# A softmax over the diagonal of a batched product: one joint load, one early maximum, one early read and a fifth store at the end of the kernel

## The chip, the cores and the metric

The kernel runs on one core of one Trainium2 chip. The metric is the device time of one execution in microseconds. The profiled span (from the program's first instruction to its last) is about 2 us shorter than that time. In the lines of profiles, DVE is VectorE, ACT is ScalarE and SP the engine that issues the loads; a q behind the name is the engine's queue, where separate waits stand; "issue" is time in which an engine waited for nothing that the profile shows; L83 is a line of the kernel (here the products by row, with their sums).

## The reference

```python
B, N, D = 8, 4096, 512          # x and y: [8, 4096, 512] float32
gram = np.matmul(x, y.transpose(0, 2, 1))
diag = np.diagonal(gram, axis1=1, axis2=2)
diag = diag - diag.max(axis=-1, keepdims=True)
exp = np.exp(diag)
return exp / exp.sum(axis=-1, keepdims=True)
```

Only the diagonal is wanted: for each of 8 x 4096 rows one dot product of 512 elements, then a softmax over 4096 dots. 134 MB are read and 0.13 MB written.

## The kernel before

Four batches form a set; their 4 x 4096 dots lie in a tile `diag[i]` of 128 partitions (32 to a batch) x 128 columns. A step `t` works on 32 columns ("rows" of x and y in each partition, 64 KB). In the code P is 128 partitions, C 128 columns, R 32 rows of a step, W 2, and G the 32 partitions of a batch. Steps 0 to 5 use large products and reduces. The last two steps use `dots`: one VectorE instruction a row, product and sum together. The last step, which the change is about, loads its rows in pieces of 16, 8, 4, 2, 1, 1.

```python
def largest(out, d):
    nc.vector.tensor_reduce(out=out, in_=d, axis=X, op=Alu.max)

def exps(i, d):                                    # softmax, first half
    mxp = small.tile([P, 1], f32, name=f"mxp{i}")
    largest(mxp, d)
    nmx = over_quadrant(f"nmx{i}", mxp, Alu.max, negate=True)     # over the 32 partitions of a batch
    sump = small.tile([P, 1], f32, name=f"sump{i}")
    nc.scalar.activation(out=res[i], in_=diag[i][:, :C], func=Act.Exp, bias=nmx, scale=1.0, accum_out=sump)
    return sump
# ... normalize(i, sump): sum over the quadrant, reciprocal, multiply res[i] ...

# steps 0 to 5: 30 of the 32 rows are summed by VectorE, the last two (W) by ScalarE:
    sums(t, 0, R - W)
    sums_act(t, R - W, W)
# ...
t += 1                                             # the last step
r0 = 0
for n in (16, 8, 4, 2, 1, 1):
    load_x(t, r0, n)
    load_y(t, r0, n)
    if r0 == 0:
        largest(diag[1][:, C : C + 1], diag[1][:, : C - R])
    if r0 == R - 2:
        largest(diag[1][:, C + 1 :], diag[1][:, C - R : C - 2])
    dots(t, r0, n)
    r0 += n

for p in range(0, P, G):                           # first set, in 4 stores
    nc.sync.dma_start(out=ov[0, p : p + G, :], in_=res[0][p : p + G, :])
normalize(1, exps(1, diag[1][:, C - 2 :]))         # 2 dots and 2 early maxima
nc.scalar.dma_start(out=ov[1], in_=res[1])
```

Transfers take eight completion counters in turn; each issue waits until the transfer eight before it has landed (the last y is issued at 304.05 us; the load eight before it landed at 303.99).

## Time and profile before

| | before |
|---|---|
| time, median of 3 runs at first | 321.22 us |
| profiled span | 319.2 us |
| y of the last step's 16 rows lands | 294.19 us |
| last y row lands | 314.15 us |
| last row's product starts | 314.24 us |
| exponential starts | 315.48 us |
| last multiply ends, last store lands | 316.73, 318.34 us |

Read it from the end: the data stream ends at 314.15 us, and then one chain of small instructions on VectorE and ScalarE and one store lead to 319.2. Beside that chain only the four stores of the first set still land, by 314.89. The lines are shown and read in the prediction below.

### The profile page before, as it was taken

Reading aid. Unit: us, or ns where it says so; the run is one execution under the profiler, and the core shown is the slowest. Engines: PE = TensorE matmul, PEld = TensorE weight load, DVE = VectorE, ACT = ScalarE, POOL = GpSimd, SP = SyncE. Lnnn points to the kernel's source line nnn. Section 1 sums busy time; section 2 is a strip of 40 time slices with the busy share of each in tenths; the row PEclk is TensorE's granted clock in tenths of the full one; section 3 lists DMA queues with packets and bytes.
Section 4 is the critical chain, followed back from the end, with each engine's and each line's share of the span. In section 5 each row is a group of like instructions: output and inputs, shape, how many; then the busy total and the mean of one; then the engine's idle time right before and its main releaser. Section 6 shows DMA issues by size and latency. Waiting matters only on the chain.

```text
span 319.2 us, 318 instructions
## 1 busy us (share of the span) xinstructions
DVE 242.8 (76%) x158; ACT 26.9 (8%) x35; POOL 0.2 (0%) x4
## 2 busy tenths in 40 slices
DVE  0000079994899939999399994999949999993995
ACT  1000030100301003010110103001030100000000
POOL 0000000000000000000000000000000000000000
DMA  9999999999999999999999999999999899999992
GB/s 394 394 394 509 411 394 493 427 394 427 493 394 394 517 402 394 493 427 394 435 485 394 394 517 402 394 493 427 394 427 493 378 411 444 412 452 409 421 410 100
DMA packets 4226, 134.36 MB, mean 421 GB/s; under 512 B 513, under 2 KB 769, under 8 KB 1537
## 3 DMA queue, kind: packets, MB, share of 16 engines
q1 hardware_dynamic: 4080, 134.29, 97.8%
q10 hardware_dynamic: 144, 0.07, 0.1%
q14 instruction: 2, 0.01, 0.0%
HBM read 134.22 MB, written 0.13 MB: 421 GB/s over the span
## 4 chain that ended last, share of the span: by engine, by line
DMA 61%; DVE 36%; issue 2%; SPq 0%; ACT 0%; DVEq 0%; ACTq 0%
DMA ys<-in_y_dram 61%; DVE xs L70 27%; DVE xs L83 5%; DVE diag L73 4%; SPq L63 0%; DVE res L111 0%; ACT res L104 0%; DVE nmx L91 0%; DVE sum L91 0%; DVE rc L110 0%; DVE mxp L97 0%; SPq L66 0%; DVEq L70 0%; DVEq L83 0%; ACTq L104 0%
## 5 line engine op out<-in xcount | busy, mean ns | idle before, releaser
L70 DVE TENSOR_TENSOR xs<-xs,ys 128x13312 f32<-128x13312 f32 x6 | 84.1, 14025 | 67.1 <-DMA ys<-in_y_dram 67.1
L73 DVE TENSOR_REDUCE diag<-xs 128x30 f32<-128x15360 f32 x6 | 96.9, 16153 | 0.2
L83 DVE SCALAR_TENSOR_TENSOR xs<-xs,ys 128x512 f32<-128x512 f32 x64 | 39.7, 686 | 5.5 <-DMA ys<-in_y_dram 5.5
L116 ACT ACTIVATE side<-ys 128x3072 f32<-128x3072 f32 x6 | 16.6, 2764 | 123.6 <-DMA ys<-in_y_dram 123.6
L70 DVE TENSOR_TENSOR xs<-xs,side 128x3072 f32<-128x3072 f32 x6 | 20.1, 3350 | 0.0
L78 ACT ACTIVATE xs<-xs 128x512 f32<-128x512 f32 x12 | 7.5, 621 | 88.2 <-DVE xs L70 88.2
L104 ACT ACTIVATE res<-diag,nmx 128x128 f32<-128x128 f32 x2 | 0.8, 401 | 76.6 <-DVE nmx L91 76.6
L83 DVE DVE_READ_ACCUMULATOR xs<-xs,ys 128x1 f32 x64 | 5.2, 82 | 0.0
L78 ACT ACTIVATION_READ_ACCUMULATOR xs<-xs 128x1 f32 x12 | 2.2, 187 | 0.0
L116 ACT ACT_TABLE_LOAD x1 | 1.3, 1283 | 0.7 <-PEq L162 0.7
L91 DVE TRANSPOSE_TENSOR_REDUCE sum<-sump 128x1 f32<-128x32 f32 x2 | 0.4, 207 | 0.6 <-ACT res L104 0.6
L111 DVE TENSOR_SCALAR res<-res,rc 128x128 f32<-128x128 f32 x2 | 0.6, 286 | 0.1
L97 DVE TENSOR_REDUCE mxp<-diag 128x1 f32<-128x128 f32 (+1 forms) x2 | 0.4, 222 | 0.1
L97 DVE TENSOR_REDUCE diag<-diag 128x1 f32<-128x96 f32 (+1 forms) x2 | 0.4, 218 | 0.1
L91 DVE TRANSPOSE_TENSOR_REDUCE nmx<-mxp 128x1 f32<-128x32 f32 x2 | 0.4, 211 | 0.1
L110 DVE RECIPROCAL rc<-sum 128x1 f32<-128x1 f32 x2 | 0.3, 163 | 0.1
L104 ACT ACTIVATION_READ_ACCUMULATOR res<-diag,nmx 128x1 f32 x2 | 0.4, 187 | 0.0
L162 POOL MEMSET const-uint8-127<- 128x1 uint8 x1 | 0.1, 103 | 0.0
L162 POOL MEMSET const-bfloat16-1.0<- 128x1 bf16 x1 | 0.1, 102 | 0.0
L162 POOL MEMSET const-float32-0.0<- 128x1 f32 x1 | 0.1, 99 | 0.2 <-issue 0.2
L162 POOL MEMSET const-float32-1.0<- 128x1 f32 x1 | 0.1, 99 | 0.0
## 6 DMA issues: line engine op xcount, KB each, us to landing
ys<-in_y_dram SPq DMA_DIRECT2D x3, 4096.0 KB, 15.1
xs<-in_x_dram SPq DMA_DIRECT2D x1, 4096.0 KB, 15.2
xs<-in_x_dram SPq DMA_DIRECT2D x1, 2048.0 KB, 19.7
ys<-in_y_dram SPq DMA_DIRECT2D x1, 2048.0 KB, 20.0
xs<-in_x_dram SPq DMA_DIRECT2D x1, 1024.0 KB, 22.1
ys<-in_y_dram SPq DMA_DIRECT2D x1, 1024.0 KB, 22.6
xs<-in_x_dram SPq DMA_DIRECT2D x1, 512.0 KB, 23.5
ys<-in_y_dram SPq DMA_DIRECT2D x1, 512.0 KB, 23.9
```

Of the source, the lines that this page charges most:

```text
L70: nc.vector.tensor_tensor(out=xt, in0=xt, in1=yt, op=Alu.mult)
L73: nc.vector.tensor_reduce(out=dots_of(t, r0, n), in_=rows(t, r0, n), axis=X, op=Alu.add)
L78: nc.scalar.activation(out=row, in_=row, func=Act.Copy, accum_out=dots_of(t, r, 1))
L83: nc.vector.scalar_tensor_tensor(out=xt, in0=xt, scalar=1.0, in1=ys[:, r, :], op0=Alu.mult, op1=Alu.mult, accum_out=dots_of(t, r, 1),)
L91: nc.vector.tensor_reduce(out=got, in_=column.to_broadcast([P, G]), axis=X, op=op, negate=negate, apply_transpose=True)
L97: nc.vector.tensor_reduce(out=out, in_=d, axis=X, op=Alu.max)
L104: nc.scalar.activation(out=res[i], in_=diag[i][:, :C], func=Act.Exp, bias=nmx, scale=1.0, accum_out=sump)
L110: nc.vector.reciprocal(out=rc, in_=total)
L111: nc.vector.tensor_single_scalar(out=res[i], in_=res[i], scalar=rc, op=Alu.mult)
L116: nc.scalar.activation(out=side, in_=ys[:, R - K :, :], func=Act.Copy)
L162: nc = _bacc.Bacc("TRN2", target_bir_lowering=False, num_devices=1)
```

## The change

The intent is to shorten the end: the x of rows 30 and 31 comes in one load, so that the last row waits for one transfer; the two early maxima become one, so that the final maximum takes three columns; ScalarE reads its own earlier sums once (into a tile `met` that nobody uses), so that its exponential need not wait for them; the first set is stored in five pieces and not in four.

```diff
-    diag = [small.tile([P, C + 2 * i], f32, name=f"diag{i}") for i in range(B // Q)]
+    diag = [small.tile([P, C + i], f32, name=f"diag{i}") for i in range(B // Q)]
@@ the last step
     for n in (16, 8, 4, 2, 1, 1):
-        load_x(t, r0, n)
+        if r0 < R - 1:
+            load_x(t, r0, max(n, 2))
         load_y(t, r0, n)
-        if r0 == 0:
-            largest(diag[1][:, C : C + 1], diag[1][:, : C - R])
         if r0 == R - 2:
-            largest(diag[1][:, C + 1 :], diag[1][:, C - R : C - 2])
+            largest(diag[1][:, C:], diag[1][:, : C - 2])
         dots(t, r0, n)
         r0 += n
 
-    for p in range(0, P, G):
-        nc.sync.dma_start(out=ov[0, p : p + G, :], in_=res[0][p : p + G, :])
+    met = small.tile([P, C - R], f32, name="met")
+    nc.scalar.activation(out=met, in_=diag[1][:, : C - R], func=Act.Copy)
+
+    for p, n in ((0, G), (G, G), (2 * G, G), (3 * G, G // 2), (3 * G + G // 2, G // 2)):
+        nc.sync.dma_start(out=ov[0, p : p + n, :], in_=res[0][p : p + n, :])
```

## The prediction

> **What bounds the kernel now.** I read the page first, for the engines' shares and the DMA row.
>
> ```profile
> span 319.2 us, 318 instructions
> DVE 242.8 (76%) x158; ACT 26.9 (8%) x35; POOL 0.2 (0%) x4
> ...
> DMA  9999999999999999999999999999999899999992
> HBM read 134.22 MB, written 0.13 MB: 421 GB/s over the span
> ```
>
> The DMA engines are at 90% or more in 38 of 40 slices: the kernel is a stream of 134 MB, and VectorE (76%) mostly waits for it. All the change's edits lie in the last step, behind the last loads, so what counts is the end of the chain of waits. The same chain cut to 283 to 317 us:
>
> ```profile
> 283.95 20.04 DMA ys<-in_y_dram
> ...
> 304.05 10.10 DMA ys<-in_y_dram
> 314.15 0.03 issue
> 314.18 0.02 DVEq L83
> 314.20 0.04 issue
> 314.24 0.71 DVE xs L83 x2
> ...
> 315.39 0.02 issue
> 315.41 0.02 ACTq L104
> 315.43 0.05 issue
> 315.48 0.07 ACT res L104
> ```
>
> The last y row lands at 314.15; VectorE's queue spends 0.09 us on two waits, then takes the last row at 314.24. After the negated maximum (315.39), ScalarE's queue spends 0.08 us on a wait before the exponential starts at 315.48. Now the timeline of VectorE over that stretch:
>
> ```profile
> 312.97 0.18 DVE L97 TENSOR_REDUCE diag<-diag 128x1 f32<-128x30 f32 x1
> 313.08 0.68 DVE L83 SCALAR_TENSOR_TENSOR xs<-xs,ys 128x512 f32<-128x512 f32 x1
> 313.68 0.08 DVE L83 DVE_READ_ACCUMULATOR xs<-xs,ys 128x1 f32 x1
> 314.24 0.69 DVE L83 SCALAR_TENSOR_TENSOR xs<-xs,ys 128x512 f32<-128x512 f32 x1 [0.48 <-DMA ys<-in_y_dram]
> ```
>
> VectorE is almost the bound here: it is idle only 0.48 us before the last row. Whatever the DMA gains, no more than about that can be won. Is the last load late because it was issued late? It waited until 304.05 for the landing of the load eight before it (the program has eight completion counters in turn). But the views of DMA issues, one short window each, give for the last four loads:
>
> ```profile
> xs<-in_x_dram SPq DMA_DIRECT2D x1, 256.0 KB, 24.2
> ys<-in_y_dram SPq DMA_DIRECT2D x1, 256.0 KB, 18.6
> xs<-in_x_dram SPq DMA_DIRECT2D x1, 256.0 KB, 14.4
> ys<-in_y_dram SPq DMA_DIRECT2D x1, 256.0 KB, 10.1
> ```
>
> With issues at 288.05, 294.26, 299.15 and 304.05 they land at about 312.21, 312.89, 313.55 and 314.15 (the second decimals from the counters' updates in the trace): one each 0.60 to 0.68 us, however early issued. Even the last stood 10 us in a full queue. Issue time is no constraint.
>
> **What the Trainium skill says.** "DMA: Bandwidth & Descriptors", section "Queues, rings and completion order": on each DMA engine descriptors are consumed in ring order. The trace agrees: the four landings above are in issue order. So a store issued behind the last load can't delay its data. The same page, "Why small descriptors are slow", gives a fixed overhead per packet of some 3 cycles. The packet records agree that small packets are dearer: 2 KB takes a median of 87 ns, 4 KB 160, against 174 for two of 2 KB. "Perfetto Trace Analysis", section "Identifying Dependency Chains", says that an instruction which waits on several engines may get separate semaphore instructions in front. The trace has them: ScalarE's of 17 ns at 315.41, VectorE's of 21 ns at 314.18. "ScalarE: Activation LUTs", section "What ACT_TABLE_LOAD costs", puts an activation with immediate scale and bias at 186 ns + 0.833 ns an element; the 3072-element copies in this trace took 2764 ns against 2745 by that formula.
>
> **The change part by part.**
>
> One load for x of rows 30 and 31. Two loads of 128 packets of 2 KB become one of 4 KB; the bytes are equal. The two old ones raised the landing time from 311.53 (the y pair before) by 0.68 + 0.66 = 1.34 us in sum; the existing 4 KB loads land 1.28 to 1.29 apart (308.96, 310.24, 311.53). So 0.05 to 0.06 us less data time. But the order changes from x30 y30 x31 y31 to x30-31 y30 y31, so row 30 now has to wait for both x rows: the joint x lands at 311.53 + 1.29 = 312.82, y30 0.67 later at 313.49 (before: 312.89), y31 0.62 later (before: 0.60) at 314.11 (before: 314.15). So row 30 loses 0.6 us, which was its lead, and row 31 wins 0.04.
>
> The waits in front of the rows. Before, row 31 waited for its own x and its own y: a separate wait, then one in the instruction, 314.15 to 314.24 = 0.09. After, x came with row 30, and row 31 needs one wait in the instruction. What that costs is read from the 16-row group, where the separately awaited load was already there: y landed at 294.19, the first product began at 294.22, 0.025. For row 30 the joint x gets the counter that x30 had (the separate wait) and y30 the one that it had (in the instruction); x lands first, so row 30 starts at 313.49 + 0.025 = 313.515. A row takes 0.613 from start to start when nothing is awaited (312.24 minus 311.63). Row 31 then starts at the later of 313.515 + 0.613 = 314.13 and 314.11 + 0.025 = 314.135. Against 314.24 that is 0.11 us earlier. The DMA and VectorE arrive together, so a faster arrival of y31 alone would bring nothing more.
>
> The maximum. The reduce over 96 columns (0.25 us at 288.93) goes, in idle time ahead of a 5.04 us wait: worth nothing. That over 30 (183 ns) becomes one over 126. From 183 ns for 30 and 253 for 96 a column costs 1.06 ns, so about 285 ns, 0.10 more, and it also waits for ScalarE's old sums (landed 60 us before). It starts at about 312.97 to 313.0 and ends by 313.29. Row 30 can't start before 313.515, so this lies in a new idle stretch: 0. The final reduce takes 3 columns and not 4, some 1 ns.
>
> ScalarE's read of its own sums. A copy of 96 columns, by the skill's formula (an estimate) 266 ns, once. The waits here are by region and not by whole tile: at 253.08 ScalarE's row sums began while VectorE's reduce into other columns of the same tile ran. So the copy waits only for columns finished at 288.8 and runs then, on an engine idle until 315.4. It takes over the wait for ScalarE's own old writes, and the last exponential keeps one wait, on VectorE's result. Start delay before: 315.394 to 315.477 = 0.083. With a single wait in the instruction: VectorE's products ended at 253.05 and ScalarE started at 253.075, 0.02 us. Gain 0.06 us, all on the path, because nothing else goes on there.
>
> Five stores. The removal of a load shifts the counters by one, so a fifth store keeps the last store of the second set behind the counter of a load that landed at about 312.8, long before its issue at 316.77. The stores go behind y31 in the ring. Before, the four landed at 314.3 to 314.9, 0.19 apart; five will be done by about 315.1, with the last store landing at 318.34. Off the path: 0.
>
> **Sum.** 0.11 (row 31) + 0.06 (ScalarE) = 0.17 us; 321.22 - 0.17 = 321.05.
>
> **The rivals.** First: the last load was late by its issue, and earlier issue (299.1 and not 304.05) lets it land early enough to close VectorE's idle time. For: the chain does show its wait for an older landing. Against: even spacing of landings and DMA shares near 1 until 313. It would give up to 0.48 + 0.06, so about 320.7. Second: the joint x load holds up row 30, so that VectorE does rows 30 and 31 after the data in series, and the gain of the single wait is lost. If y31 lands only after row 30 is done or VectorE restarts with 0.09 us twice, row 31 starts at 314.20 to 314.25 and only ScalarE's 0.06 remains: 321.16. This is the likeliest way to miss, for my sum assumes that two arrivals meet within 0.03 us. Third: the wider reduce comes onto the path, if row 30's data is there before 313.29; it costs at most 0.10, about 321.15. Against: 4 MB of queue cannot shorten by that much. Fourth: the copy of the sums is made to wait for the last rows, if the dependence is on the whole tile. It would start at about 315.0 and end at 315.3, still ahead of 315.37: no loss, but it is a near thing, up to 0.1 (321.2).
>
> **Range and chances.** The sure term is ScalarE's 0.06; the row's 0.11 may be anything from 0 to 0.15. The three runs before spread over 0.08 us, and another execution or another chip may add 0.1. So 321.05, and 320.85 to 321.25 should hold it 8 times in 10. A move of 2% is 6.4 us, and everything behind the last load's landing is 5 us in all: faster by 2% I give 0.004, slower 0.004 (only a deadly new stall could), the same 0.992.
>
> **What would show it.** In the changed kernel's timeline: row 30's product near 313.5 with an idle gap before it, named as y's landing; row 31 near 314.13 with a gap under 0.05; a reduce of 126 columns of about 285 ns ending before 313.3; ScalarE's copy at about 288.9; no queue wait of ScalarE in the chain at 315.3, and 0.02 us between the negated maximum and the exponential. In the DMA issues: the last y issued at about 299.15, landing near 314.1, so some 15 us. A landing under 313.9 would make the first rival right; a copy after 314 the fourth; a gap over 0.08 us between the last landing and row 31 would make the wait term wrong.

## The result, and the profile after

The changed kernel took 320.93 us (median of 6 runs, 320.83 to 321.22); the kernel before 321.25 (median of 6, 321.14 to 321.56). The ratio is 0.9990 with a 95% interval of 0.9978 to 1.0003. By the rule of 2% the two are the same, and the 0.32 us between the medians is about twice the 0.17 predicted.

The page of the changed kernel, its first lines (span, and busy time of the engines with their instruction counts):

```profile
span 319.1 us, 316 instructions
...
DVE 242.6 (76%) x157; ACT 27.1 (9%) x36; POOL 0.2 (0%) x4
```

One more ScalarE instruction (36 for 35) and one less on VectorE (157 for 158). The span fell by less than 0.1 us in this execution (319.07 for 319.15, by the trace). The chain that ended last, from 294 us on (start, duration, what):

```profile
294.36 19.20 DMA ys<-in_y_dram
313.56 0.02 issue
313.58 1.35 DVE xs L83 x4
...
315.37 0.02 issue
315.39 0.02 ACT res L104
```

Two things differ from the chain before. The chain no longer enters VectorE through a separate wait and the last y, but through the y of row 30, with both rows (four instructions, two products and two reads of their sums) behind it. And no separate wait of ScalarE stands between the negated maximum and the exponential. VectorE's timeline over the same stretch, and ScalarE's one new instruction:

```profile
313.15 0.28 DVE L97 TENSOR_REDUCE diag<-diag 128x1 f32<-128x126 f32 x1
313.58 0.69 DVE L83 SCALAR_TENSOR_TENSOR xs<-xs,ys 128x512 f32<-128x512 f32 x1
314.20 0.08 DVE L83 DVE_READ_ACCUMULATOR xs<-xs,ys 128x1 f32 x1
314.22 0.69 DVE L83 SCALAR_TENSOR_TENSOR xs<-xs,ys 128x512 f32<-128x512 f32 x1
```

```profile
288.88 0.28 ACT L144 ACTIVATE met<-diag 128x96 f32<-128x96 f32 x1 [34.51 <-DVE xs L83]
```

Row 31 starts 0.02 us after the read of row 30's sum began. Where a next row waits for nothing, the two start together (before, 312.24 and 312.24 for such a pair), so 0.02 us of wait are all that is left. The wide reduce ends at 313.43, and row 30 starts 0.15 us later: it does not delay anything. The copy runs at 288.88, in idle time. The DMA issues of the last two y rows (KB, us from issue to landing; issued at 294.36 and 299.26 us):

```profile
ys<-in_y_dram SPq DMA_DIRECT2D x1, 256.0 KB, 19.2
ys<-in_y_dram SPq DMA_DIRECT2D x1, 256.0 KB, 14.9
```

The last y is issued 4.8 us earlier than before and waits 4.8 us longer in the queue: it lands at 314.20.

Absolute times of two executions can't be compared to 0.1 us. All kernels issue the same loads up to the 16-row y, and in their profiled executions it landed anywhere between 294.05 and 294.60 us. So the end is best counted from that landing. From the trace records of the profiled executions (us; "last y" and "row 31" counted from the landing of the 16-row y; "ScalarE" from the end of the negated maximum to the exponential, which begins 0.013 before the moment that the prediction counts from, so that its 0.083 and 0.02 are 0.096 and about 0.035 here; "rest" from the start of row 31 to the end of the last multiply; "outside" is time minus span, exact for the profiled execution; e6, e9, e10 and b1 are left out, and told of below):

```
kernel                        last y   row 31   wait   ScalarE   rest   outside
before                        19.957   20.049   0.092   0.096    2.490   2.117
changed                       19.899   19.922   0.023   0.035    2.427   1.951
e1_again (changed)            19.927   19.950   0.023   0.034    2.428   1.962
e2_joint                      19.889   19.913   0.024   0.093    2.491   2.125
e3_reads_own                  19.974   20.067   0.093   0.035    2.430   1.953
e4_four_stores                19.896   19.919   0.023   0.035    2.431   1.947
e5_one_max                    19.964   20.057   0.093   0.094    2.492   2.134
e7_two_x                      19.957   20.050   0.093   0.035    2.430   1.965
d1_idle_copy                  19.980   20.074   0.094   0.095    2.492   1.965
d2_two_copies                 19.902   19.926   0.024   0.034    2.430   1.786
```

("wait" is from the landing of the last y to the start of row 31.) The span explains 0.13 us at row 31 and 0.06 at ScalarE. The last column is what the prediction didn't have at all: with the change, the part of the time that lies outside the span is 0.17 us shorter. The experiments were made to settle the first two and to find what the third belongs to.

### The profile page after: what moved, and what is told of

Same layout as the page of the kernel before. It is cut to its first block, busy times and chain, and to the rows that moved or that the text cites. A ratio compares the mean times of both kernels' runs of the same rounds, so it can differ in the third digit from the quotient of the medians.

```text
span 319.1 us, 316 instructions
## 1 busy us (share of the span) xinstructions
DVE 242.6 (76%) x157; ACT 27.1 (9%) x36; POOL 0.2 (0%) x4
## 4 chain that ended last, share of the span: by engine, by line
DMA 62%; DVE 35%; issue 2%; SPq 0%; ACT 0%; DVEq 0%
DMA ys<-in_y_dram 62%; DVE xs L70 27%; DVE diag L73 4%; DVE xs L83 4%; SPq L63 0%; DVE res L111 0%; DVE nmx L91 0%; DVE sum L91 0%; ACT res L104 0%; DVE rc L110 0%; DVE mxp L97 0%; SPq L66 0%; DVEq L70 0%
```

## The experiments

My theory: in the span, the gain is the joint load (a shorter landing and one wait less) plus ScalarE's wait, and the other two parts are worth nothing. Rivals: the gain belongs to the order of the loads, or to the fifth store; or, for the part outside the span, to the wait that is gone rather than to the extra instruction. Every kernel gave a correct result. All were timed in 5 rounds; "before" is the kernel before in the same rounds (9 runs each). The sets ran on four chips (e1 to e4 on one; d1, d2, e6 and e7 on another; e5, e9 and e10 on a third; b1 on a fourth), so a time is compared with the kernel before of its own set. "Outside" is here the mean over all timed runs, whose spans are known to 0.1 us.

| kernel | median us | before | ratio, 95% interval | outside |
|---|---|---|---|---|
| e1_again | 320.97 | 321.30 | 0.9989 (0.9977 to 1.0002) | 1.97 |
| e2_joint | 321.07 | 321.30 | 0.9992 (0.9979 to 1.0004) | 2.14 |
| e3_reads_own | 321.05 | 321.30 | 0.9994 (0.9981 to 1.0006) | 1.96 |
| e4_four_stores | 321.24 | 321.30 | 0.9998 (0.9984 to 1.0012) | 1.94 |
| d1_idle_copy | 321.20 | 321.37 | 0.9993 (0.9980 to 1.0005) | 1.96 |
| d2_two_copies | 320.77 | 321.37 | 0.9978 (0.9965 to 0.9992) | 1.78 |
| e7_two_x | 321.07 | 321.37 | 0.9989 (0.9976 to 1.0001) | 1.96 |
| e6_joint_y | 321.72 | 321.37 | 1.0010 (0.9997 to 1.0022) | 1.95 |
| e9_nine | 320.92 | 321.25 | 0.9988 (0.9975 to 1.0000) | 1.78 |
| e10_many | 320.79 | 321.25 | 0.9986 (0.9972 to 0.9999) | 1.79 |
| e5_one_max | 321.42 | 321.25 | 1.0004 (0.9991 to 1.0016) | 2.14 |
| b1_early_bias | 320.53 | 321.30 | 0.9978 (0.9965 to 0.9992) | 1.79 |

The 36 runs of the kernel before in these four sets have 2.13 outside. Their spans scatter with a standard deviation of 0.19 us. So a time alone can't settle a tenth of a microsecond; the columns of the table above and "outside", which repeat to 0.04 or better among the kernels of one kind listed there, can (e10_many, not listed, has its row 31 at 19.876, which makes it 0.07 for that column).

### e1_again: the changed kernel, unaltered

> The changed kernel again, unaltered, to see how large the difference really is. My prediction's theory (0.11 us from one wait less and a smaller packet cost at the last row, 0.06 us from ScalarE's start, nothing else) expects 0.17 us less than the kernel before, that is 0.9995 of it, in span as in time. The rival, that there is a further gain that my sum lacks (the first measurement showed 0.32 us between medians), expects 0.30 us or more again, 0.9990.

Measured: a median 0.33 us under the kernel before, and by the means 0.32 again (321.35 to 321.03). The rival is right: there is a further gain. The chain in the span repeats the first profile (row 31 at 19.950, ScalarE 0.034), so the further gain is not in the last step's chain. Outside: 1.97 against 2.11 for the nine runs of before.

### e2_joint: the joint load of x alone

```diff
-        load_x(t, r0, n)
+        if r0 < R - 1:
+            load_x(t, r0, max(n, 2))
@@
-    for p in range(0, P, G):
+    for p, n in ((0, G), (G, G), (2 * G, G), (3 * G, G // 2), (3 * G + G // 2, G // 2)):
```

> The kernel before with the joint load of x for rows 30 and 31 (and five stores, so that the counters fall as in the changed kernel), its two early maxima and ScalarE's wait kept. My theory: the last row starts some 0.03 us after its y landed and not 0.09, and about 0.1 us earlier counted from the landing of the 16-row y; ScalarE still has 0.08 us from the negated maximum to the exponential. So 0.11 us less than the kernel before. The rival that row 30's later start eats the gain: last row no earlier than before, 0.00.

Measured: row 31 at 19.913, 0.14 us earlier than before. Its chain:

```profile
313.41 1.33 DVE xs L83 x4
...
315.20 0.02 ACTq L104
```

The entry is that of the changed kernel, and ScalarE's separate wait is still there. So the joint load does all of the first term and nothing of the second; outside stays at 2.14. The rival that row 30's delay eats the gain falls.

### e3_reads_own: ScalarE's read of its sums alone

```diff
+    met = small.tile([P, C - R], f32, name="met")
+    nc.scalar.activation(out=met, in_=diag[1][:, : C - R], func=Act.Copy)
+
     for p in range(0, P, G):
```

> The kernel before with ScalarE's one read of its own sums alone. My theory: the separate wait in ScalarE's queue ahead of the last exponential goes, 0.02 us from negated maximum to exponential and not 0.08, so 0.06 us less; the copy runs at about 288.9 us. The rival that the whole gain of the changed kernel comes from the loads: 0.00 here, with the wait still there.

Measured: ScalarE's start delay fell from 0.096 to 0.035 us, as expected, and row 31 stayed at 20.067. In its chain VectorE still waits twice, ScalarE no more:

```profile
314.08 0.02 DVEq L83
...
314.15 0.71 DVE xs L83 x2
...
315.32 0.02 ACT res L104
```

And the part outside the span is 1.96: the third term comes with this one copy.

### e4_four_stores: the changed kernel with four stores

```diff
-    for p, n in ((0, G), (G, G), (2 * G, G), (3 * G, G // 2), (3 * G + G // 2, G // 2)):
-        nc.sync.dma_start(out=ov[0, p : p + n, :], in_=res[0][p : p + n, :])
+    for p in range(0, P, G):
+        nc.sync.dma_start(out=ov[0, p : p + G, :], in_=res[0][p : p + G, :])
```

> The changed kernel with the first set stored in four pieces again. The last store then takes the completion counter of a load of two y rows that landed at about 311.6 us, still long before it is issued. My theory: same time as the changed kernel within 0.05 us, last store issued 0.3 us after the last product as before. The rival that the fifth store is needed for the gain: slower than the changed kernel by 0.1 us or more, with a wait at the last store or at the end.

Measured: up to the last multiply as the changed kernel, and the last store is issued 0.03 us after it. But from the end of the last multiply to the end of the span it is 2.487 us and not 2.423. The program's ending waits for the counters one by one, and the trace has two of these waits behind the last store's landing (at 318.43 and 318.50) where the changed kernel has one. The view of the ending's line from the landing on, first here, then in the changed kernel:

```profile
L175 SPq EVENT_SEMAPHORE  x2: 28/28/28, 318.4 to 318.5; - x2
```

```profile
L175 SPq EVENT_SEMAPHORE  x1: 28/28/28, 318.3 to 318.3; - x1
```

With four stores the last store takes the counter before the last one in that order, so one wait more follows its landing. So the fifth store is worth 0.065 us. The expectation of "the same within 0.05" just missed; the rival's 0.1 or more is seen in the medians (321.24 for 320.97), but the earlier part scatters by more than that: the 16-row y landed 0.41 us later in this profiled execution than in e1_again's. By an estimate from their times and this chain, its five runs had that landing at 294.35 to 294.74, and e1_again's at 294.04 to 294.49. So a loss beyond the 0.065 is neither shown nor excluded: whether this kernel's stream ends later by chance or by a cause stays open.

### e5_one_max: the single early maximum alone

```diff
-        if r0 == 0:
-            largest(diag[1][:, C : C + 1], diag[1][:, : C - R])
         if r0 == R - 2:
-            largest(diag[1][:, C + 1 :], diag[1][:, C - R : C - 2])
+            largest(diag[1][:, C:], diag[1][:, : C - 2])
```

> The kernel before with the one early maximum over 126 columns alone. My theory: the longer reduce (284 ns and not 183, and a second wait) starts row 30 some 0.1 to 0.25 us later, but row 31 still waits for its y: last row, span and time as the kernel before, 0.00; outside the span 2.12. The rival that the reduce is on the path: 0.1 us or more slower.

Measured: the longer reduce and its extra wait do delay row 30, by 0.18 us counted from the 16-row landing, but row 31 starts at 20.057, as before (20.049). The timeline shows the slack left:

```profile
313.36 0.28 DVE L97 TENSOR_REDUCE diag<-diag 128x1 f32<-128x126 f32 x1
...
314.55 0.69 DVE L83 SCALAR_TENSOR_TENSOR xs<-xs,ys 128x512 f32<-128x512 f32 x1 [0.30 <-DMA ys<-in_y_dram]
```

VectorE still waits 0.30 us for the last y. The median is 0.17 us above before; the chain and the part outside (2.134) show no cause for it, and the 16-row y of the profiled execution landed 0.30 later than before's. The part is worth nothing, as predicted.

### e7_two_x: the joint load taken apart, order kept

```diff
-            load_x(t, r0, max(n, 2))
+            for r, m in ((r0, n),) if n > 1 else ((r0, 1), (r0 + 1, 1)):
+                load_x(t, r, m)
@@ and four stores, so that the counters fall as before
```

> The changed kernel with the joint load of x taken apart into two loads of one row, both still ahead of the two y rows (and four stores, so that the counters fall as before the change). It takes the 4 KB packets and the single wait away and keeps the order x, x, y, y. My theory: row 31 starts 0.09 us after its y landed (two waits again) and the landing itself some 0.06 us later counted from the 16-row y: last row 0.1 to 0.13 us later than in the changed kernel, so the whole first term of my sum is gone. Rival that the order makes the gain: last row as in the changed kernel.

Measured: last y at 19.957 and row 31 at 20.050, within 1 ns of the kernel before. Its chain has the gap back between the rows:

```profile
313.96 0.64 DVE xs L83
314.61 0.04 issue
314.65 0.71 DVE xs L83 x2
```

So the order of the loads is worth nothing. Of the first term, about half is the landing (19.957 to about 19.90, by 4 KB packets for 2 KB) and half the single wait (0.093 to 0.023). The time of 321.07 still beats before by 0.30, as it has ScalarE's 0.06 and the 0.17 outside.

### e6_joint_y: y of the last two rows in one load too

```diff
-        load_y(t, r0, n)
+        if r0 < R - 1:
+            load_y(t, r0, max(n, 2))
```

> The changed kernel with y of the last two rows in one load too. Both rows then become ready with the last landing, some 0.06 us earlier than y31 before, and VectorE has to do them in series behind it. My theory (row 30's lead hides one row's product, 0.61 us): last row starts 0.61 us after the landing, so 0.5 to 0.6 us slower than the changed kernel. Rival that smaller packets cost more than the lead is worth: faster by 0.05 us.

Measured: 321.72, 0.35 us over before and, by the ratios to before, 0.67 over the changed kernel (1.0010 less e1_again's 0.9989, times 321). VectorE does both rows behind the one landing:

```profile
314.24 0.69 DVE L83 SCALAR_TENSOR_TENSOR xs<-xs,ys 128x512 f32<-128x512 f32 x1 [0.81 <-DMA ys<-in_y_dram]
...
314.86 0.69 DVE L83 SCALAR_TENSOR_TENSOR xs<-xs,ys 128x512 f32<-128x512 f32 x1
```

Row 31 starts 0.642 us after the landing instead of 0.023. With the 0.06 us of e4's counter order, which this kernel has too (2.479 us from the last multiply to the end), that is the measured loss. Here joining the loads pays only as long as row 30's lead is kept.

### d1_idle_copy: a ScalarE copy that has nothing to do with the wait

```diff
+    idle = small.tile([P, C - R], f32, name="idle")
+    nc.scalar.activation(out=idle, in_=res[0][:, : C - R], func=Act.Copy)
+
     for p in range(0, P, G):                       # of the kernel before
```

> All kernels with ScalarE's extra copy so far have some 1.95 us between the time and the profiled span, those without it 2.11 to 2.14. Here the kernel before gets a ScalarE copy of the same size that reads the finished first set and not the sums, so that the separate wait ahead of the last exponential must stay. Theory that one more ScalarE instruction, whatever it does, shortens the part outside the span: 1.95 outside, 0.08 us from negated maximum to exponential, in all 0.16 us less than the kernel before. Rival that it belongs to the wait that is gone: 2.12 outside and no gain at all.

Measured: 1.96 outside, and the separate wait is still in its chain:

```profile
315.62 0.02 ACTq L104
```

ScalarE's delay is 0.095 as before, and row 31 is at 20.074. So the part outside the span shortens with one more ScalarE copy, whether or not it meets the sums. The rival falls. Time: 0.17 us under before by the medians, with nothing changed in the span's end.

### d2_two_copies: a second one in the changed kernel

The same two lines, added to the changed kernel behind its own copy.

> The changed kernel with that second ScalarE copy as well. If each further ScalarE instruction shortens the part outside the span, 1.79 us outside; if it is a matter of where the instruction list ends (a step), 1.95 or back to 2.12. In the span nothing: the exponential 0.02 to 0.04 us after the negated maximum, span as the changed kernel's within 0.1 us.

Measured: 1.78 outside, another 0.17 us, and the chain in the span as the changed kernel's. With 320.77 us and a ratio of 0.9978 (0.9965 to 0.9992) this kernel is below the kernel before with the whole interval, and its median is 0.2 under the changed kernel's (of other rounds). Its page counts one instruction more on ScalarE (37 for 36).

### e9_nine and e10_many: eight and 24 further copies

```diff
+    idle = small.tile([P, 8], f32, name="idle")
+    for r in range(8):                              # 24 in e10_many
+        nc.scalar.activation(out=idle[:, r : r + 1], in_=res[0][:, r : r + 1], func=Act.Copy)
```

> The changed kernel with eight further ScalarE copies of one column, in ScalarE's idle time behind its read of the sums. One copy more took 0.17 us off the part outside the span, two took 0.34 to 0.36. If each further instruction takes 0.17 us off, 1.95 - 8 x 0.17 = 0.6 us outside, and some 319.6 us in all; if there is a floor, a value between 0.6 and 1.78 outside that tells it. In the span no change.

> The same with 24 further copies. If it goes on for ever, the part outside would be below zero, which can't be: so a floor, the same as with eight or lower; or, if what counts is the place of the list's end in some block, a part outside that has risen again, up to 2.1. In the span no change: the copies end about 5 us after 289, well ahead of 315.

Measured: 1.78 and 1.79 outside. Counted by instructions there is a floor, and two extra ones reach it: 2.13, 1.96, 1.78, 1.78, 1.79 for 0, 1, 2, 9 and 25 more than before. So neither "each one more" nor "a matter of the place in some block" in the form that rises again is seen up to 25.

A rival to the instruction count was left untested. Every kernel with one extra copy also has one extra tile for ScalarE to write (`met` or `idle`), and d2_two_copies, e9_nine, e10_many and b1_early_bias all have two, since the eight and the 24 copies share one tile. Counted by such tiles, 0, 1 and 2 of them give 2.13, 1.96 and 1.78 to 1.79, and no floor is needed. Two copies into one tile would tell the two apart; no run has that.

Still open is the mechanism, and even on which side of the span it lies: the trace holds only the program's own instructions. Instruction counts of other engines moved too in these kernels (two fewer on VectorE and one on SyncE in the changed kernel, one fewer on each in e2_joint) and e2_joint's outside did not; adding instructions to other engines wasn't tried.

### b1_early_bias: what a shorter chain would bring

```diff
# of d2_two_copies
-        if r0 == R - 2:
-            largest(diag[1][:, C:], diag[1][:, : C - 2])
+        if r0 == 0:
+            largest(diag[1][:, C:], diag[1][:, : C - R])
+            nmx1 = over_quadrant("nmx1", diag[1][:, C:], Alu.max, negate=True)
@@
-    normalize(1, exps(1, diag[1][:, C - 2 :]))
+    sump = small.tile([P, 1], f32, name="sump1")
+    nc.scalar.activation(out=res[1], in_=diag[1][:, :C], func=Act.Exp, bias=nmx1, scale=1.0, accum_out=sump)
+    normalize(1, sump)
```

> The kernel with two ScalarE copies, and the negated maximum of the last set taken early, over the 96 columns that are known at 289 us, in VectorE's idle time; the late maximum and its quadrant step go from the end. The result is the same in exact arithmetic, and for this input in float too, but an input whose last quarter tops the rest by some 88 would overflow: an experiment, not a kernel to ship. My theory: everything behind the last row is one chain, so 0.17 + 0.22 + 0.04 = 0.43 us go in full: the exponential starts some 0.74 us after the last row's start plus one wait and not 1.17; 1.78 outside the span; 320.35 us. Rival that the end of the last row and the exponential are bound by something else: under 0.2 us gained.

Measured: in the chain just that. From row 31's start to the end of the last multiply it is 1.992 us for d2_two_copies' 2.430, 0.44 less, because the exponential follows the last row at once:

```profile
313.76 1.33 DVE xs L83 x4
315.09 0.02 issue
315.11 0.03 ACT res L153
```

The time shows less of it: 320.53, only 0.24 under d2_two_copies by the medians, which are of different rounds and chips. By the ratios, each to the kernel before of its own rounds, nothing of it is seen (0.9978 for both). So the gain of 0.44 is shown in the chain and not in the time. In the profiled execution the 16-row y landed 0.24 us later (294.447 for 294.210). The other four of the five runs, by the same estimate as for e4_four_stores, had it at 294.26 to 294.89. All kernels issue the same loads up to there and the landing scatters between all of them, but whether this one is late by chance or by a cause stays open. It is the fastest median. It is not one to ship, since it gives up the true maximum as the bias of the exponential.

## Why the prediction was right or wrong

The time of 320.93 us lies in the range (320.85 to 321.25), and the class is the one given 0.992. That it lies there is owed in part to luck: the range is 0.40 us wide, wider than the whole gain, and had room for a term of 0.17 that the sum lacks. Step by step:

- **The joint load.** Right in mechanism, small misses in size. Row 30's y landed 0.56 us later counted from the 16-row y (0.60 predicted) and row 31's 0.03 to 0.07 earlier (0.04). That the two arrivals meet held: VectorE could have begun row 31 at 314.20, its y landed at 314.20, and the row began at 314.22.
- **The waits in front of the rows.** Right: 0.092 to 0.023 us for row 31 (0.09 to 0.025 predicted). e7_two_x, which takes the single wait and the larger packet back, loses the whole term.
- **Sum of the two**: about 0.14 us (mean of row 31 over the four profiles without the joint load, before, e3, e5 and d1: 20.062; over the changed kernel, e1, e2, e4 and d2: 19.926) against 0.11.
- **The maximum.** Right to count 0; 284 ns for the predicted 285. It ended at 313.43 and not before 313.3: its two waits put its start 0.19 us after the last read of a sum began, where the old reduce started 0.12 after. One effect wasn't foreseen: without the early reduce, the first product of the 16-row group starts 0.08 us after its y and not 0.02. That is absorbed by VectorE's later idle time.
- **ScalarE's read.** In the span right: 0.061 us for 0.06, at 288.88 us for 288.9, with waits by region. The copy took 282 ns for the estimated 266.
- **Five stores.** Counted as 0, which holds for the change as it stands; but the reason given, the counter of an early landing, was not the point. Without the fifth store 0.065 us would have been lost in the ending's waits (e4_four_stores).
- **The sum.** This is the step that fell short. "0.11 (row 31) + 0.06 (ScalarE) = 0.17 us" took the time before and subtracted what happens in the span, as if the 2 us outside were fixed. They are not: 0.17 us more came off there, with the extra ScalarE copy (d1_idle_copy shows that a copy which has nothing to do with the sums does it too; by what mechanism, and whether by the instruction or its new tile, stays open). With it the sum is 0.14 + 0.06 + 0.17 = 0.37 us; the medians differ by 0.32 and 0.33.
- **The rivals.** The first (an earlier issue lands earlier) is refuted: 4.8 us earlier in issue, 4.8 us longer in the queue. The second (only ScalarE's gain remains) is refuted by e2_joint. The third and fourth didn't occur. One reading was loose from the start: VectorE does not "mostly wait" for the stream; it is idle for 24% of the span, though nearly all of that (72.6 us) is waiting for y.

## What to carry to other kernels

Where the last row waits for two transfers, let one of them come earlier and jointly, so that one wait is left; but keep the transfers of the last pieces small enough that each piece's work hides behind the next landing. On an engine that will have to wait for its own old results and for a fresh one, make it meet the old ones in idle time. And at the level of tenths of a microsecond, take the span and the time outside it apart for every run before explaining a difference: here nearly half of it was in neither the data stream nor the chain.

## What the Trainium skill lacked or had wrong

- "Perfetto Trace Analysis", section "Identifying Dependency Chains", tells that separate semaphore instructions are inserted, not what one costs: with it, VectorE's product started 0.092 us after the landing, without it 0.023; ScalarE's exponential 0.096 and 0.035 us after the negated maximum. So 0.06 to 0.07 us each, though the instruction itself is 17 to 21 ns long.
- I found no page that says that the part of the time outside the program's own span shortens with further ScalarE copies: 2.13, 1.96, 1.78, 1.78, 1.79 us for 0, 1, 2, 9 and 25 more (or for 0, 1, 2, 2 and 2 further tiles). "Runtime: NRT & Kernel Launch", section "The ~15µs preamble/postamble breakdown", calls a gap of about 6.2 us between two total times "kernel-invariant"; that is another quantity, but the one here is not invariant.
- "DMA: Bandwidth & Descriptors", section "Why small descriptors are slow", gives a fixed overhead of about 3 cycles a packet, which at that page's 850 MHz is an estimated 3.5 ns, and 32 bytes of metadata besides. Here 2 KB took a median of 87 ns and 4 KB 160 in the kernel before, 85 and 161 in the changed one, which puts the fixed part at an estimated 2 x 87 - 160 = 14 ns, or 2 x 85 - 161 = 9. Eight packets fewer on each of 16 engines would then save an estimated 0.07 to 0.11 us; the last landing came some 0.06 us earlier.
- I found no page on the order in which a program's ending waits for the completion counters, nor that a last store behind the wrong one costs a further wait: 2.487 for 2.423 us from the last multiply to the end.
